# Seven block products for eight in the last MLP pass of a hybrid encoder layer

## The chip, the cores and the metric

The kernel runs on one core of one Trainium2 chip. The metric is the device time in microseconds of one execution. The program has five compute engines that work through their own instruction queues in order: TensorE (PE, with its weight loads shown apart as PEld), VectorE (DVE), ScalarE (ACT), GpSimd (POOL) and SyncE (SP), which in this kernel issues most of the transfers.

## The reference

The input `x` has 2048 tokens of 1024 features, float32. The layer is an RMS norm and a projection into attention (8 heads of 64, three dilation patterns) and a convolution branch, a cross-attention over 256 memory tokens, an MLP, and a closing RMS norm. The part that the change touches is the end:

```python
u = rmsnorm(h, norm_mlp_g[l]) @ w_up[l]            # 1024 -> 4096
h = h + jnp.square(jax.nn.relu(u)) @ w_down[l]     # 4096 -> 1024
return rmsnorm(h, norm_final_g)
```

## The kernel before, in words

Each float32 operand of a large product is split into a high part (rounded to the type that TensorE reads in one pass, `F32R`) and a low part, the difference. A product is then three matmuls, high x high, high x low, low x high. `mm3` (L198 to L201) issues them, one line each, so every large product shows up at L199, L200 and L201. `wsplit2` (L187) makes the two parts of a weight: ScalarE copies the raw weight to the high part (L190), VectorE subtracts (L191).

After a first stage (input projection, convolution and the first attention), the 2048 tokens go through the rest in four passes of 512, `post(p)` (L1219), p = 0 to 3: output projection, cross-attention, MLP, closing norm. While pass p runs, the attention and the convolution of pass p + 1 are woven in between (`weave`, L92 and L1398); pass 3 has nothing woven in. In all passes activations are held by columns: features on the 128 partitions, tokens along the free dimension. The residual stream is eight tiles `hs[m]` of 128 features x 512 tokens.

The MLP of a pass goes in eight groups `fg` of 512 hidden units. For each group:

- four chunks `c` of 128 hidden units. `wpost` (L1089) loads a 512 KB piece of `w_up` and splits it; 8 x 3 matmuls with the weight stationary and 512 tokens streaming give the tile `up`; VectorE applies relu and the norm's factor (L1321), ScalarE squares (L1322) and copies the high part `hhh` (L1323), VectorE makes the low part `hhl` (L1324);
- four pieces of `w_down`, each 512 hidden units x 256 output features, 512 KB, loaded and split the same way. `down` (L1331) makes two tiles `dn` from each, 4 x 3 matmuls per tile, and VectorE adds each to the residual `h` (L1339).

A group is thus 96 matmuls up and 96 down. Raw weights go through two slots (`raw`, two buffers), split weights through four (two in each of two pools, `wp` and `wq`, taken by turns). All weights are issued on SP's queue; a raw slot is free for the next load when the low part has been made from it. The `up` and `dn` tiles take turns in three accumulator banks.

In pass 3 the last group's second product is done in two halves of 256 tokens, so that the closing norm of the first half (`final`, L1354) can go on beside the second. `final` sums the squares over features with matmuls against ones (`rstd_from`, L1170), takes the reciprocal root (`rstd_col`, L169, with GpSimd's power at L177), multiplies by the gain (L1360), turns the tiles by transposes on TensorE (L1367), scales on VectorE or ScalarE (L1371, L1369) and stores.

The order of each queue is not written out by hand alone: a planner takes the program's order and a timeline of its own, and places the instructions and their waits; the order in which `post` and the woven generators yield decides what it sees first.

Of the kernel before, what the change touches and what calls it, by code (L numbers as in the profile page):

```python
# [21 lines left out]
P = 128  # L22
# [21 lines left out]
def f(ap):  # L44
    return ap.bitcast(F32)


def hybrid_layer(ctx, tc, A, out):
# [70 lines left out]
    bscr = dr.tile([KC, P, KC, P], F32, name="bscr")  # L119

# [77 lines left out]
    def mm3(o, lh, ll, rh, rl, first, end):  # L198
        PE.matmul(o, lh, rh, start=first, stop=False)  # L199
        PE.matmul(o, lh, rl, start=False, stop=False)  # L200
        last["pe"] = PE.matmul(o, ll, rh, start=False, stop=end)  # L201
# [894 lines left out]

    wout = {}
# [57 lines left out]
    def ytile(q, k, name, dtype=F32R):  # L1155
        return yp.tile([P, 512], dtype, tag=f"y{q}{k}", name=name)
# [62 lines left out]
    def post(p):  # L1219
# [88 lines left out]
        end = p == NG - 1  # L1308
        for fg in range(FG):
# [16 lines left out]
            if fg == FG - 1:  # L1326
                fsum = ssum_tile(f"f{p}")
                if not end:
                    load_cat(p + 1, 0)

            def down(mp2, t, w, wh, wl):  # L1331
                sl = slice(t, t + w)
                for e in range(2):
                    m = 2 * mp2 + e
                    es = slice(P * e, P * e + P)
                    pt = ps("mm", "dn")[:, 0:w]
                    for k in range(4):
                        mm3(pt, wh[:, k, es], wl[:, k, es], hh["h", k][:, sl], hh["l", k][:, sl], k == 0, k == 3)
                    last["dve"] = DVE.tensor_tensor(hs[m][:, sl], hs[m][:, sl], pt, op=ALU.add)  # L1339
                    if fg == FG - 1:  # L1340
                        add_sq(hs[m][:, sl], fsum[:, sl], m == 0)

            wd = []
            for mp2 in range(4):
                wd.append(wpost(wcols(w_down, mp2 * 256, 256, (4 * fg, 4 * fg + 4)), f"d{p}{fg}_{mp2}", (P, 4, 256)))
                if fg == FG - 1 and end:
                    continue
                down(mp2, 0, 512, *wd[-1])
                yield


        fin = {}

        def final(t, w):  # L1354
            r = rstd_from(fsum[:, t:t + w])
            sl = slice(t, t + w)
            for k in range(KC):
                if t == 0:
                    fin[k] = ytile("h", k, f"fin{p}_{k}", F32)
                DVE.tensor_scalar(fin[k][:, sl], hs[k][:, sl], gain("final", k), None, op0=ALU.mult)  # L1360
            for j in range(w // P):
                c0 = t + P * j
                for g in range(2):
                    ot = ytile("l", 2 * (c0 // P) + g, f"ot{p}{c0}{g}", F32)
                    pt = ps("T", "ot")
                    for i in range(4):
                        PE.transpose(pt[:, P * i:P * i + P], fin[4 * g + i][:, c0:c0 + P], ident)  # L1367
                    if g:
                        ACT.activation(ot, pt, AF.Copy, scale=r[:, j:j + 1])  # L1369
                    else:  # L1370
                        DVE.tensor_scalar(ot, pt, r[:, j:j + 1], None, op0=ALU.mult)  # L1371
                    dma(out[0, 512 * p + c0:512 * p + c0 + P, 512 * g:512 * (g + 1)], ot)
                yield

        if end:
            for t in range(0, 512, 256):
                for mp2 in range(4):
                    down(mp2, t, 256, *wd[mp2])
                yield from final(t, 256)
        else:  # L1380
            load_cat(p + 1, 1)
            yield from final(0, 512)
# [75 lines left out]
```

## Time and profile before

| what | value |
|---|---|
| median of 3 executions | 2888.27 us (2886.27 to 2889.25) |
| the profiled execution | 2888.26 us |
| its span, first to last instruction | 2886.5 us |
| mean granted TensorE clock | 0.994 |
| instructions | 41313 |
| TensorE, VectorE, ScalarE, GpSimd busy | 98%, 64%, 40%, 16% of the span |
| DMA traffic | 433.74 MB, mean 150 GB/s |
| MLP of pass 0, 1, 2, 3 (approximate stretches) | 905 to 1295, 1451 to 1842, 1997 to 2387, 2529 to 2876 us |

Times in a row are microseconds unless marked ns. A row of a group of instructions names line, engine and operation, then what it writes from what it reads, its shapes and count; after the bar come busy time and the mean of one in ns, and then the idle time of the engine before it with what ended that. A matmul's recorded length is longer than its share of TensorE's time, since the next one starts before it ends; counts over a stretch tell the pace. In a row of waits, "A <- B: t, n, m" says that A waited for B t us in total, n times, m at the longest.

### The profile page before, as it was taken

The page shows a single profiled execution, that of the slowest core. Times are in us where ns is not written, and L with a number is a line of the kernel's source. Part 1 is how long each engine was busy: PE and PEld are TensorE (multiplying, and loading weights), DVE is VectorE, ACT ScalarE, POOL GpSimd, SP SyncE. Part 2 cuts the span into 40 slices and gives each one's busy share as a digit, 9 for nine tenths or more (in the row PEclk, how much of TensorE's full clock was granted, in tenths as well). Part 3 has the DMA queues.
Part 4 walks back from the last instruction along what each step waited for, and adds up shares of the span by engine and source line. Part 5 has one row for each costly group of instructions (what it writes and reads, how often), then busy time and mean ns, then how long its engine had stood idle before and what let it go on. Part 6 is the DMA issues. An engine that isn't in the chain of part 4 may idle for free.

```text
span 2886.5 us, 41313 instructions
## 1 busy us (share of the span) xinstructions
PE 2826.6 (98%) x15628; PEld 2376.2 (82%) x15628; DVE 1857.6 (64%) x3306; ACT 1166.3 (40%) x1988; POOL 458.0 (16%) x469
## 2 busy tenths in 40 slices
PE   8999999998999999999999999999999999999999
PEld 7878899887788888888888888888888888888887
DVE  5636535565789776557887765689876555544445
ACT  5633211475554333434543343444333433432233
POOL 1336421122102011200012012002011200000000
PEclk9999999999999999999999999999999999999999
DMA  8979845799734444554444446534543445333332
GB/s 264 295 173 228 202 132 131 182 256 247 205 102 131 135 133 123 168 160 145 121 130 130 138 117 192 175 96 128 142 127 109 139 132 175 93 90 101 96 95 74
DMA packets 598632, 433.74 MB, mean 150 GB/s; under 512 B 191550, under 2 KB 524786, under 8 KB 597921
## 3 DMA queue, kind: packets, MB, share of 16 engines
q1 hardware_dynamic: 558256, 408.21, 50.2%
q10 hardware_dynamic: 37952, 16.88, 2.4%
q0 software_dynamic: 2224, 6.01, 0.6%
q8 instruction: 123, 2.02, 0.3%
q14 instruction: 77, 0.62, 0.1%
HBM read 339.89 MB, written 91.11 MB: 149 GB/s over the span
## 4 chain that ended last, share of the span: by engine, by line
PE 82%; DVE 9%; DMA 5%; issue 2%; ACT 2%; POOL 1%; SPq 1%; POOLq 0%; DVEq 0%; ACTq 0%
PE dn L199 8%; PE dn L200 8%; PE dn L201 8%; PE up L199 7%; PE up L200 7%; PE up L201 7%; PE lin L199 4%; PE lin L201 4%; PE lin L200 4%; DVE cacc L216 3%; PE o L199 2%; PE o L200 2%; PE o L201 2%; PE xs L199 2%; PE xs L201 2%; PE xs L200 2%
## 5 line engine op out<-in xcount | busy, mean ns | idle before, releaser
L199 PE MATMUL dn<-hhh,whi_d 128*128 128x512 f32 (+1 forms) x1056 | 402.8, 392 | 7.2 <-DVE h L1339 6.1
L200 PE MATMUL dn<-hhl,whi_d 128*128 128x512 f32 (+1 forms) x1056 | 403.4, 385 | 1.1 <-DVE hhl L1324 1.1
L199 PE MATMUL up<-mh,whi_u 128*128 128x512 f32 x1024 | 402.9, 393 | 0.5 <-DVE rl L1321 0.5
L201 PE MATMUL dn<-hhh,wlo_d 128*128 128x512 f32 (+1 forms) x1056 | 402.6, 384 | 0.0
L200 PE MATMUL up<-ml,whi_u 128*128 128x512 f32 x1024 | 399.4, 390 | 1.0 <-DVE ml L1214 0.9
L201 PE MATMUL up<-mh,wlo_u 128*128 128x512 f32 x1024 | 399.7, 391 | 0.0
L216 DVE SCALAR_TENSOR_TENSOR cacc<-cu,cw,cacc 128x512 f32<-128x512 f32 x480 | 389.0, 811 | 5.5
L190 ACT CAST whi_d<-raw_d 128x1024 fp32r<-128x1024 f32 x128 | 134.6, 1052 | 418.1 <-PE up L200 378.6
L1339 DVE TENSOR_TENSOR h<-h,dn 128x512 f32<-128x512 f32 (+1 forms) x264 | 172.3, 667 | 162.9 <-PE dn L201 161.7
L190 ACT CAST whi_u<-raw_u 128x1024 fp32r<-128x1024 f32 x128 | 134.4, 1050 | 327.2 <-PE dn L200 304.1
L1321 DVE SCALAR_TENSOR_TENSOR rl<-up,ssumx 128x512 f32<-128x512 f32 x128 | 88.0, 690 | 256.9 <-PE up L201 252.6
L199 PEld LDWEIGHTS dn<-hhh,whi_d 128*128 128x128 f32 x1056 | 198.1, 189 | 47.5 <-DVE h L1339 10.2
L201 PEld LDWEIGHTS dn<-hhh,wlo_d 128*128 128x128 f32 x1056 | 198.8, 188 | 39.7
L200 PEld LDWEIGHTS dn<-hhl,whi_d 128*128 128x128 f32 x1056 | 199.3, 189 | 37.4 <-DVE hhl L1324 2.0
L200 PEld LDWEIGHTS up<-ml,whi_u 128*128 128x128 f32 x1024 | 192.4, 188 | 40.1 <-DVE ml L1214 2.3
L201 PEld LDWEIGHTS up<-mh,wlo_u 128*128 128x128 f32 x1024 | 192.2, 188 | 40.3
L199 PEld LDWEIGHTS up<-mh,whi_u 128*128 128x128 f32 x1024 | 192.4, 188 | 38.5 <-DVE rl L1321 0.9
L774 ACT ACTIVATE sm<-sm,o 128x256 f32<-128x256 f32 (+1 forms) x384 | 160.1, 466 | 126.3 <-DVE o L773 125.9
L773 DVE CUSTOM_DVE_ANT_0 sm<-s,mask 128x256 f32<-128x256 f32 (+1 forms) x384 | 128.5, 375 | 83.5 <-PE s L999 39.4
L191 DVE TENSOR_TENSOR wlo_u<-raw_u,whi_u 128x1024 fp32r<-128x1024 f32 x128 | 158.4, 1237 | 32.7 <-ACT whi_u L190 32.4
L191 DVE TENSOR_TENSOR wlo_d<-raw_d,whi_d 128x1024 fp32r<-128x1024 f32 x128 | 163.2, 1275 | 23.8 <-ACT whi_d L190 23.7
L177 POOL TENSOR_TENSOR nr<-st_v,mhalf 128x4 f32<-128x4 f32 (+1 forms) x13 | 13.0, 997 | 839.2 <-DVE st_v L173 839.2
(403 smaller groups left out, 6320.9 us busy)
## 6 DMA issues: line engine op xcount, KB each, us to landing
raw_u<-in_w_up_dram SPq DMA_DIRECT2D x128, 512.0 KB
raw_d<-in_w_down_dram SPq DMA_DIRECT2D x128, 512.0 KB
raw_o<-in_w_out_dram SPq DMA_DIRECT2D x32, 512.0 KB
raw_a<-ascr SPq DMA_DIRECT2D x32, 512.0 KB
raw_b<-bscr SPq DMA_DIRECT2D x32, 512.0 KB
k<-kscr SPq DMA_DIRECT2D x24, 512.0 KB
k<-kscr SPq DMA_DIRECT2D x8, 1152.0 KB
xn<-in_x_dram SPq DMA_DIRECT2D x32, 256.0 KB
```

The costliest lines, as they stand in the source:

```text
L177: POOL.tensor_tensor(dst, v, mhalf.to_broadcast([P, v.shape[1]]), op=ALU.pow)
L190: ACT.copy(hi, raw)
L191: (lo_eng or DVE).tensor_tensor(lo, raw, f(hi), op=ALU.subtract)
L199: PE.matmul(o, lh, rh, start=first, stop=False)
L200: PE.matmul(o, lh, rl, start=False, stop=False)
L201: last["pe"] = PE.matmul(o, ll, rh, start=False, stop=end)
L216: DVE.scalar_tensor_tensor(acc, u[:, t:t + 512], cw[:, c, t:t + 1], acc, op0=ALU.mult, op1=ALU.add)
L773: last["dve"] = DVE.tensor_tensor_reduce(dst, so, mask[:, 256 * m:256 * m + nk], 1.0, 3e38, ALU.add, ALU.min, mn)
L774: last["act"] = ACT.activation(dst, dst, AF.Exp, bias=mn, scale=-1.0)
L1321: last["dve"] = DVE.scalar_tensor_tensor(r, pt, 0.0, rsb, op0=ALU.max, op1=ALU.mult)
L1339: last["dve"] = DVE.tensor_tensor(hs[m][:, sl], hs[m][:, sl], pt, op=ALU.add)
```

## The change

Three things change.

Pass 3's MLP is a function of its own, `last_mlp`. The sum is held by rows: tokens on the partitions, 1024 features along the free dimension, in two tiles `acc` of four banks' width. The residual's 32 blocks are turned into rows by transposes during the first two chunks of the first group (`to_rows`). In the second product the hidden activations become the stationary operand, and 512 columns of the weight stream.

For the first seven groups, the second product is done as a product of 2 x 2 blocks with seven block products for eight. The activations' blocks are halves of the tokens by halves of the group's hidden units; the weight's are halves of the hidden units by alternate blocks of 128 output features. `parts` makes the activations' blocks and their sums S1 to S4 from each chunk, split into high and low parts. `seven` runs the products in the order A11, A12, S2, S1, S3, S4, A22. Some go on adding in a bank whose content was already added to the rows: the pair of banks X takes A11, S2, S3 and A22, the pair Y takes A12, and the pair Z (the same banks as Y) takes S1 and S4. After each product VectorE adds both tiles of its pair to the rows. The next group's first chunk is computed before the seven products. The eighth group is a plain product, 512 wide, with its rows closed one tile of 128 tokens after another: square and total on ScalarE, reciprocal root, one scaling by factor and gain on VectorE, store from SP's and ScalarE's queues.

The four sums of weight blocks that the seven products need are made in passes 0 to 2: pass p does them for the groups with `fg % 3 == p`, below 7. When a `w_down` piece has been split, VectorE overwrites the raw tile's four blocks with differences, and the tile is written to DRAM (`dscr`). In pass 3 each product's weight is loaded as two transfers of 256 KB, from `w_down` (three of the seven) or from `dscr` (four).

```diff
+    dscr = dr.tile([7, 4, P, 4, 256], F32, name="dscr")
...
+    def wdown(p, fg, m):
+        raw = wp.tile([P, 4, 256], F32, tag="raw", name=f"raw_d{p}{fg}_{m}", bufs=2)
+        dma(raw, wcols(w_down, m * 256, 256, (4 * fg, 4 * fg + 4)))
+        n = turn_w[0]
+        turn_w[0] += 1
+        w = wsplit2(wq if n % 4 > 1 else wp, raw, f"d{p}{fg}_{m}", shape=(P, 4, 256))
+        if fg < 7 and fg % 3 == p:
+            (b11, b12), (b21, b22) = ([raw[:, 2 * a:2 * a + 2, P * b:P * b + P] for b in range(2)] for a in range(2))
+            for o, x, y in ((b11, b12, b11), (b12, b22, b12), (b22, b22, b11), (b21, b21, b22)):
+                DVE.tensor_tensor(o, x, y, op=ALU.subtract)
+            dma(dscr[fg, m], raw)
+        return w
...
+    def last_mlp(hs, y, rsb):
+        FG, p = 8, NG - 1
+        banks.update(up=(4, 5, 6, 7), ux=(0, 1), uy=(2, 3), tr=(0, 1, 2, 3))
+        acc = [xp_.tile([P, 4, 512], F32, tag=f"x{q}0", name=f"rows{q}") for q in "hl"]
+        grow = aq.tile([P, D], F32, tag="ld", name="gain_row")
+        dma(grow, A["norm_final_g"].unsqueeze(0).to_broadcast([P, D]))
...
+        def to_rows(g):
+            t, c = divmod(g, 2)
+            pt = ps("tr", f"hT{g}")
+            for i in range(4):
+                PE.transpose(pt[:, P * i:P * i + P], hs[4 * c + i][:, P * t:P * t + P], ident)
+            ACT.copy(row(t)[:, 512 * c:512 * c + 512], pt)
+
+        def split(t, src):
+            ACT.copy(t[0], src)
+            DVE.tensor_tensor(t[1], src, f(t[0]), op=ALU.subtract)
+
+        def hidden(fg, c):
+            wh, wl = wpost(wcols(w_up, fg * 512 + c * P), f"u{p}{fg}_{c}")
+            pt = ps("up", "up")
+            for k in range(KC):
+                mm3(pt, wh[:, k, :], wl[:, k, :], y["h", k], y["l", k], k == 0, k == KC - 1)
+                if fg == 0 and c < 2 and k % 2:
+                    to_rows(4 * c + k // 2)
+            r = tmp("rl") if c else cv.tile([P, 512], F32, tag="vr", name="rl", bufs=2)
+            last["dve"] = DVE.scalar_tensor_tensor(r, pt, 0.0, rsb, op0=ALU.max, op1=ALU.mult)
+            ACT.activation(r, r, AF.Square)
+            return r
...
+        def parts(rs_, c):
+            r, j = rs_[c], c % 2
+            lo, hi = r[:, 0:256], r[:, 256:512]
+            if c < 2:
+                split([x[:, j] for x in A1], lo)
+                DVE.tensor_tensor(lo, lo, hi, op=ALU.subtract)
+                split([x[:, j] for x in S3], lo)
+            else:
+                r0 = rs_[j]
+                split([x[:, j] for x in A2], r)
+                DVE.tensor_tensor(r0[:, 256:512], r0[:, 256:512], hi, op=ALU.add)
+                DVE.tensor_tensor(r0[:, 0:256], hi, r0[:, 0:256], op=ALU.subtract)
+                split([x[j] for x in S12], r0)
+                DVE.tensor_tensor(lo, lo, r0[:, 0:256], op=ALU.subtract)
+                split([x[:, j] for x in S4], lo)
+
+        def seven(fg):
...
+            for n, (key, w, pts, more, t0, c0) in enumerate((
+                    ("A11", direct(0, 0), X, False, 0, 0), ("A12", direct(1, 0), Y, False, 0, 0),
+                    ("S2", sums(1, 1), X, True, 0, 1), ("S1", sums(0, 0), Z, False, 2, 1),
+                    ("S3", sums(0, 1), X, True, 2, 1), ("S4", direct(1, 1), Z, True, 0, 1),
+                    ("A22", sums(1, 0), X, True, 2, 0))):
+                raw = wp.tile([P, 2, 512], F32, tag="raw", name=f"raw_d{p}{fg}{n}", bufs=2)
+                for j in range(2):
+                    dma(raw[:, j].rearrange("p (m c) -> p m c", m=4), w[j])
...
+                for t in range(2):
+                    for j in range(2):
+                        mm3(pts[t], at[key](0, j, t), at[key](1, j, t), wh[:, j], wl[:, j], not more and j == 0, j == 1,
+                            more)
+                    a = row(t0 + t).rearrange("p (m h c) -> p m h c", m=4, h=2)[:, :, c0, :]
+                    last["dve"] = DVE.tensor_tensor(a, a, pts[t].rearrange("p (m c) -> p m c", m=4), op=ALU.add)
+
+        rs_ = []
+        for fg in range(FG - 1):
+            for c in range(4):
+                if c or not fg:
+                    rs_.append(hidden(fg, c))
+                parts(rs_, c)
+            rs_ = [hidden(fg + 1, 0)]
+            seven(fg)
...
+        for t in range(4):
+            for c in range(2):
+                pt = ps("tr", "dn")
+                for k in range(4):
+                    wh, wl = ws[c][k // 2]
+                    mm3(pt, *(x[:, k, P * t:P * t + P] for x in hh), wh[:, k % 2], wl[:, k % 2], k == 0, k == 3)
+                a = row(t)[:, 512 * c:512 * c + 512]
+                DVE.tensor_tensor(a, a, pt, op=ALU.add)
+                ACT.activation(tmp("sq"), a, AF.Square, accum_out=ss[:, 2 * t + c:2 * t + c + 1])
...
+            rstd_col(r[:, 0:1], sq, 1, top)
+            for c in range(2):
+                a = row(t)[:, 512 * c:512 * c + 512]
+                DVE.scalar_tensor_tensor(a, a, r[:, 0:1], grow[:, 512 * c:512 * c + 512], op0=ALU.mult, op1=ALU.mult)
+                dma(out[0, 512 * p + P * t:512 * p + P * (t + 1), 512 * c:512 * c + 512], a, nc.scalar if c else None)
```

More of the change, by code (lines that the diff above doesn't have):

```diff
@@ L1307, in post @@
         FG = 8
-        end = p == NG - 1
+        if p == NG - 1:
+            last_mlp(hs, y, rsb)
+            return
         for fg in range(FG):
@@ L1327, in post, with down @@
                 fsum = ssum_tile(f"f{p}")
[L1328 to L1332, printed above, removed]
+                load_cat(p + 1, 0)
+            def down(mp2, wh, wl):
                 for e in range(2):
@@ L1352, in post @@
+        r = rstd_from(fsum)
         fin = {}
-        def final(t, w):
-            r = rstd_from(fsum[:, t:t + w])
-            sl = slice(t, t + w)
-            for k in range(KC):
[L1358 to L1373, printed above, removed]
```

81 lines of the change are left out of this document (60 added, 21 removed).

## The prediction

> **What bounds the kernel now.** I read the page first, part 1 and part 4 (the chain that ended last).
>
> ```profile
> PE 2826.6 (98%) x15628; PEld 2376.2 (82%) x15628; DVE 1857.6 (64%) x3306; ACT 1166.3 (40%) x1988; POOL 458.0 (16%) x469
> PE 82%; DVE 9%; DMA 5%; issue 2%; ACT 2%; POOL 1%; SPq 1%; POOLq 0%; DVEq 0%; ACTq 0%
> ```
>
> TensorE is busy 98% of the span and carries 82% of the chain. A share is an average, so the stages come next: the table by stretches, the four MLP stretches in the first four rows (passes 0 to 3), then 100 us inside pass 3, and the two halves of pass 0's MLP.
>
> ```profile
> 905.00:1295.00 390.00, 386.34 (x2001) 319.21 (x2000) 269.35 (x430) 151.20 (x228) 62.31 (x60) 1.00 0.49 141
> 1451.00:1842.00 391.00, 389.48 (x2029) 322.52 (x2027) 270.98 (x436) 152.13 (x229) 62.86 (x61) 1.00 0.49 142
> 1997.00:2387.00 390.00, 386.52 (x2006) 319.28 (x2005) 267.38 (x419) 149.01 (x223) 56.67 (x57) 1.00 0.45 131
> 2529.00:2850.00 321.00, 320.52 (x1415) 263.67 (x1414) 150.80 (x181) 97.78 (x122) 1.01 (x1) 1.00 0.32 95
> 2600.00:2700.00 100.00, 100.00 (x442) 82.36 (x441) 47.60 (x56) 28.82 (x35) 0.00 (x0) 1.00 0.34 100
> 1000.00:1100.00 100.00, 97.58 (x533) 80.81 (x532) 77.39 (x125) 37.32 (x60) 14.30 (x14) 0.98 0.49 138
> 1100.00:1200.00 100.00, 100.00 (x534) 82.99 (x533) 58.24 (x103) 43.23 (x66) 19.20 (x22) 1.00 0.45 133
> ```
>
> Columns: length, then busy time and count on PE, PEld, DVE, ACT, POOL, then granted clock, DMA share, GB/s. Pass 3's MLP runs alone, with TensorE idle 0.5 us in 321, VectorE half idle and the DMA engines at a third. It is paced by the number of matmuls: 442 in 100 us is 0.226 us each (the 0.39 us of a record overlaps the next). The waits of all engines in that stretch say what is late behind TensorE.
>
> ```profile
> ACT whi_u L190 <- PE dn L200: 115.7, 28, 5.5
> PE up L199 <- DVE rl L1321: 0.5, 1, 0.5
> ```
>
> ScalarE, which makes the next weight's high part, waits for TensorE to free a buffer, up to 5.5 us: weights are ready early. So a matmul removed here is time removed, until something else becomes late.
>
> **The change, part by part.**
>
> *Fewer matmuls (a gain).* A group's second product in pass 3 takes 8 tiles x 4 k x 3 = 96 matmuls; as seven block products, 7 x 2 row tiles x 2 k x 3 = 84, again 512 wide. Seven groups lose 12 each: 84 x 0.226 = **-19.0 us**. A group falls from 192 x 0.226 = 43.4 to 180 x 0.226 = 40.7 us. That matmuls fed the other way round (activations stationary, weights streaming) keep this pace is taken from the cross-attention scores, which already run so at the same recorded length (398 ns against 393).
>
> ```profile
> L199 PE MATMUL xs<-whi_a,yh 128*128 128x512 f32 x256 | 101.5, 398 | 0.0
> L199 PE MATMUL up<-mh,whi_u 128*128 128x512 f32 x1024 | 402.9, 393 | 0.5 <-DVE rl L1321 0.5
> ```
>
> *The last group and the close.* Before, the eighth group's second product is 192 matmuls 256 wide, with transposes among them; rows of the timeline:
>
> ```profile
> 2850.69 0.28 PE L199 MATMUL dn<-hhh,whi_d 128*128 128x256 f32 x1
> ...
> 2873.27 1.03 PE L1367 MATMUL ot<-ident,fin 128*128 128x128 f32 x8
> 2874.06 0.36 PE L200 MATMUL dn<-hhl,whi_d 128*128 128x256 f32 x1
> ...
> 2876.05 0.28 PE L201 MATMUL dn<-hhh,wlo_d 128*128 128x256 f32 x1
> 2876.37 0.42 DVE L1339 TENSOR_TENSOR h<-h,dn 128x256 f32<-128x256 f32 x1
> ...
> 2878.46 0.16 DVE L173 TENSOR_SCALAR st_v<-nps 128x2 f32<-128x2 f32 x1 [0.70 <-PE nps L1174]
> ...
> 2880.01 0.75 DVE L1371 TENSOR_SCALAR ot<-ot,nr 128x512 f32<-128x512 f32 x1
> ...
> 2882.36 0.75 DVE L1371 TENSOR_SCALAR ot<-ot,nr 128x512 f32<-128x512 f32 x1 [1.59 <-PE ot L1367]
> ```
>
> First to last start is 25.4 us; 96 matmuls 512 wide take 95 x 0.226 = 21.5: **-3.9**. The 32 turns into rows come instead at the start of pass 3's MLP, among the first two up products: 8 cost 2874.06 - 2873.27 = 0.79 us, so 32 cost **+3.2**. After the last matmul starts, the old close needs 2886.5 - 2876.05 = 10.45 us. The new one: 0.4 until the sum can be read, 0.69 sum, 0.63 square with its total and 0.4 of handovers and adding two totals, 1.55 from the mean to the finished factor (2878.46 to 2880.01, GpSimd's power included), two scalings 1.45, and 3.4 from the start of the last transfer to the end (2882.36 + 0.75 to 2886.5): 8.5, so **-1.9**. It loses the column sums and transposes that wait inside the old close.
>
> *Work on VectorE and the weight ring in pass 3 (cover: TensorE's 40.7 us a group).* Rows of pass 3, by form:
>
> ```profile
> L191 DVE TENSOR_TENSOR wlo_d<-raw_d,whi_d 128x1024 fp32r<-128x1024 f32 x32 | 39.2, 1225 | 11.2 <-ACT whi_d L190 11.2
> L1339 DVE TENSOR_TENSOR h<-h,dn 128x512 f32<-128x512 f32 x56 | 37.2, 686 | 74.4 <-PE dn L201 74.4
> L190 ACT CAST whi_d<-raw_d 128x1024 fp32r<-128x1024 f32 x32 | 33.7, 1054 | 108.7 <-PE up L200 103.2 <-issue 5.5
> L1321 DVE SCALAR_TENSOR_TENSOR rl<-up,ssumx 128x512 f32<-128x512 f32 x32 | 21.9, 691 | 85.1 <-PE up L201 81.7 <-ACT ssumx L1304 3.5
> L1322 ACT ACTIVATE rl<-rl 128x512 f32<-128x512 f32 x32 | 19.9, 625 | 0.0
> L1165 DVE TENSOR_TENSOR ssumf<-ssumf,sq 128x256 f32<-128x256 f32 x14 | 5.9, 423 | 1.5 <-ACT sq L1164 1.4
> ```
>
> Per group VectorE gets 11 low parts x 1.225, 14 sums into the rows x 0.686, 4 relus x 0.69, six 256-wide ops (0.423) for chunks 0 and 1 together, and four 512-wide and eight 256-wide for chunks 2 and 3: 13.5 + 9.6 + 2.8 + 2.5 + 6.1 = 34.5 us of 40.7, 85%. In the seven products alone, 7 x (1.225 + 2 x 0.686) = 18.2 us against 84 x 0.226 = 19.0. That fits with little to spare. ScalarE needs about 20 us.
>
> Each product uses its 512 KB weight for only 12 matmuls, 2.7 us, against 24 matmuls before. The raw weights have two slots; a slot turns in: issue, landing, high part, low part. Landing is bounded by these rows (one weight issued at 2672.81, traffic over before 2677):
>
> ```profile
> 2672.81 16.86 SPq L57 DMA_DIRECT2D raw_u<-in_w_up_dram  x4
> 2674.00:2675.00 1.00, 1.00 (x6) 0.84 (x5) 0.00 (x0) 0.00 (x0) 0.00 (x0) 1.00 0.61 143
> 2675.00:2676.00 1.00, 1.00 (x6) 0.81 (x5) 0.00 (x0) 0.09 (x1) 0.00 (x0) 1.00 1.09 324
> 2676.00:2677.00 1.00, 1.00 (x6) 0.84 (x5) 0.69 (x2) 1.00 (x2) 0.00 (x0) 1.00 0.14 39
> ```
>
> About 3.7 us to land, 0.4 for the second issue (a weight is now two transfers), 1.05 + 0.2 + 1.23: 6.6 us for a slot, 3.3 us for a weight. Needed is 40.7 / 11 = 3.7 on average, and 2.7 within the burst, where four split weights and two raw ones (some 11 us of TensorE work) are in hand. Waits of 0.8 us more per slot would use up the margin. I take **+2** for pass 3; ends 0 and +40 (a slot of 8.5 us: 11 x 8.5 / 2 = 46.8 a group, 6.1 x 7 = 43).
>
> The page "SBUF — State Buffer" of the Trainium skill, section "The DMA setup-cost knee", says that a transfer pays about 2 us however small it is, and advises few large ones. By it two halves one after the other would land in some 5.2 us (my estimate from its fit) and a slot would take 8.1 us, which puts the sum near 2891. The stretch at 2675 moves 324 GB/s, and halves follow each other by one issue, so I expect the fixed parts to overlap.
>
> *Sums of weights in passes 0 to 2 (28 weights).* Four in-place 256-wide differences: 4 x 0.423 = 1.7 us of VectorE each, 47 us in all, then a 512 KB write out of the same raw slot. Cover: TensorE spends 390 / 64 = 6.1 us per weight, VectorE 269 / 64 = 4.2. In the half with the convolution (77.39 of 100) it is 4.7, and 4.7 + 1.7 = 6.4 is over 6.1. That half holds 4 of the 7 groups (0 and 3 of pass 0, 1 of pass 1, 2 of pass 2), so 16 weights run over by 0.3 us, partly within the 2.7 us that a three-bank ring of accumulators allows. The write is queued on SP, where the next raw load and the attention's loads stand behind it.
>
> ```profile
> SPq L57 <- DVE wlo_d L191: 82.2, 23, 6.3
> L191 DVE TENSOR_TENSOR wlo_d<-raw_d,whi_d x31: 1171/1226/2071, 908.0 to 1265.9; 128x1024 fp32r<-128x1024 f32 x31
> PE dn L199 <- DVE h L1339: 2.4, 1, 2.4
> ```
>
> SP already stands up to 6.3 us for a low part (first row, pass 0) without TensorE noticing (third row), and four split weights are worth 24 us, so a slot that turns some 6 us later should be absorbed. I take **+2.5**; ends 0 and +27 (those 16 weights with nothing hidden). Neither term has an end below nothing, as both only add work behind a TensorE that is already full. The planner orders every queue anew, which I price at nothing, with 2 us either way for the range.
>
> *Sum.* -19.0 - 3.9 + 3.2 - 1.9 + 2 + 2.5 = -17.1. The profiled execution took 2888.26 us (span 2886.5, 1.8 around it), equal to the median 2888.27 of the runs. **Forecast 2871 us.**
>
> **The rivals.**
>
> *A, pass 3 bound by the raw slots (slower).* Speaks for it: two slots, half the matmuls per weight, an in-order VectorE at 85%. Against: today's 5.5 us waits of ScalarE, DMA at a third. The gain without it is 21.6 us, 3.1 a group; a group must reach 43.8 us, a slot 8.0 us, before the change loses. At 8.5 us: 2866.7 + 43 + 2.5 = 2912; at 8.2, 45.1 a group, +31 and 2900.
>
> *B, VectorE's handovers pace the burst (no change).* The third, fifth and seventh products add onto banks whose last sums must be read first, and the fourth and sixth reuse the pair of two products earlier. If each of 14 sums costs 0.2 us of waiting, 18.2 + 2.8 = 21.0 against 19.0: +2 a group, 14 in all: 2883; with the chunk chain (relu, square, split) late once a group by 1 us, 2890. Against: a sum has a whole product, 2.7 us, before it is wanted.
>
> *C, the sums disturb passes 0 to 2.* 27 us unhidden gives 2866.7 + 2 + 27 = 2896. For: 6.4 against 6.1; low parts up to 2.07 us where GpSimd works. Against: only 16 weights.
>
> *D, the covers hold entirely.* 2867.
>
> **How the numbers follow.** The forecast with its own range 2864 to 2879: 0.60. D below that or at its edge, 0.05. B or a milder C, 2879 to 2894: 0.20. A, or C in full, above 2894: 0.15. A change under 0.2% (5.8 us) can't be told from none. Faster (under 2882.5): 0.60 + 0.05 + 0.08 of B's = 0.73. Same: 0.10. Slower: 0.17, A and C with the upper end of B's. The range 2862 to 2893 leaves out A and C in full and little else.
>
> **What would show it.** Right: in pass 3 a group lasts 40.7 to 41.2 us, TensorE busy over 98%, 84 matmuls fewer in seven groups, VectorE near 85%, ScalarE's waits for TensorE shorter but there; passes 0 to 2's MLP stretches within 1 us of 390 each. Wrong: TensorE waiting in the seven products for a low part or a raw weight (A), for a sum into the rows (B), or, in passes 0 to 2, for a relu, a residual sum or an attention load (C).

## The result and the profile after

The changed kernel takes 2915.56 us in the median (2910.10 to 2918.73) against 2889.06 for the kernel before in the same series: a ratio of 1.0089 [1.0074, 1.0103]. It is slower by 26.5 us, where 2871 was forecast and 2893 was the upper end of the range. The profiled execution took 2910.39 us, its span 2908.6.

The page of the changed kernel, engines and chain, answers to the first rows of the prediction:

```profile
PE 2841.5 (98%) x15440; PEld 2359.6 (81%) x15440; DVE 1975.3 (68%) x3557; ACT 1206.9 (41%) x2055; POOL 457.1 (16%) x471
PE 80%; DVE 10%; DMA 6%; ACT 2%; issue 1%; SPq 0%; POOL 0%; DVEq 0%; POOLq 0%; ACTq 0%
```

There are 188 matmuls fewer, yet TensorE is busy for 15 us longer. So they must have become slower. The table by stretches: the MLP of passes 0 to 2, that of pass 3, and 100 us inside pass 3.

```profile
900.00:1307.00 407.00, 396.26 (x2000) 320.72 (x1999) 289.36 (x477) 151.67 (x228) 61.02 (x60) 0.98 0.51 150
1468.00:1867.00 399.00, 391.67 (x2003) 320.16 (x2002) 279.92 (x464) 151.68 (x228) 62.45 (x60) 0.99 0.50 147
2028.00:2424.00 396.00, 388.88 (x1984) 317.27 (x1983) 277.17 (x446) 149.56 (x222) 56.36 (x56) 1.00 0.47 140
2571.00:2878.00 307.00, 306.57 (x1333) 249.19 (x1332) 228.64 (x337) 135.78 (x185) 0.00 (x0) 1.00 0.46 135
2700.00:2800.00 100.00, 100.00 (x435) 81.51 (x434) 76.73 (x116) 45.94 (x64) 0.00 (x0) 1.00 0.48 140
```

Two things are seen. In pass 3 TensorE is idle for 0.4 us of 307, so none of the waits that rivals A and B spoke of came; but 100 us hold 435 matmuls where they held 442: 0.230 us each, for 0.226. And the three other passes, some 390 us each before, now take 407, 399 and 396 us for the same 2000 matmuls, with TensorE idle for 7 to 11 us and the mean clock of the first two below 1.

The span can be cut by the first and the last of the small matmuls that sum the squares ahead of each MLP. They are grouped under the tile `ssumx`, with the starts of the first and the last after the three durations. Kernel before:

```profile
L1174 PE MATMUL nps<-ones,ssumx x32: 164/250/250, 901.5 to 2529.6; 128*128 128x1 f32 x32
```

Changed kernel:

```profile
L1191 PE MATMUL nps<-ones,ssumx x32: 164/250/250, 896.4 to 2567.7; 128*128 128x1 f32 x32
```

Up to the first: the head. From the first to the last: passes 0 to 2. From the last to the end: pass 3. Before 901.5 + 1628.1 + 356.9, after 896.4 + 1671.3 + 340.9. Pass 3 gained 16.0 us; passes 0 to 2 lost 43.2.

All runs in one table, cut in the same way (the ratio is to the kernel before on the same chip; where there is no interval, it was one execution). The time is the median of a kernel's executions, the three parts are those of its profiled execution, which took 2910.39 us in the changed kernel, 2894.29 in E1 and 2888.93 in E6:

| run | time, us | ratio | head + passes 0 to 2 + pass 3, us |
|---|---|---|---|
| before | 2889.06 | 1 | 901.5 + 1628.1 + 356.9 |
| changed | 2915.56 | 1.0089 [1.0074, 1.0103] | 896.4 + 1671.3 + 340.9 |
| E1 changed, tiles back in place | 2890.11 | 1.0006 [0.9989, 1.0022] | 902.4 + 1654.6 + 335.5 |
| E2 before, right side 96 bytes down | 2917.49 | 1.0096 [1.0077, 1.0114] | 906.1 + 1645.4 + 362.3 |
| E9 before, right side 64 bytes down | 2902.46 | | 907.9 + 1634.5 + 358.3 |
| E13 before, right 96 down, left 32 up | 2912.77 | | 906.5 + 1643.2 + 361.3 |
| E15 before, both sides 32 up | 2884.67 | | 898.3 + 1627.5 + 357.1 |
| E16 before, left side 96 up | 2913.52 | | 906.5 + 1642.8 + 362.4 |
| E3 E1 without sums and writes | 2866.59 | 0.9919 [0.9898, 0.9939] | 900.7 + 1628.3 + 336.2 |
| E4 E3 with the sums | 2878.74 | 0.9960 [0.9948, 0.9972] | 899.5 + 1640.6 + 336.3 |
| E5 E3 with the writes | 2868.02 | 0.9916 [0.9901, 0.9931] | 897.6 + 1631.8 + 335.8 |
| E6 E1, sums spread | 2883.71 | 0.9974 [0.9962, 0.9987] | 907.6 + 1643.7 + 335.8 |
| E7 E6, sums behind the residual adds | 2883.00 | 0.9966 [0.9954, 0.9979] | 904.2 + 1643.2 + 335.4 |
| E8 E6, write from GpSimd's queue | 2881.99 | 0.9969 [0.9958, 0.9980] | 901.6 + 1647.1 + 335.3 |
| E10 E1, sums in the late groups | 2880.85 | 0.9953 [0.9938, 0.9968] | 901.6 + 1641.9 + 335.6 |
| E11 E10, sums behind the residual adds | 2879.06 | 0.9954 [0.9940, 0.9969] | 903.3 + 1638.2 + 336.0 |
| E14 E11, no sums in pass 1 | 2883.17 | 0.9966 [0.9945, 0.9986] | 903.2 + 1643.0 + 335.5 |
| E17 E11, sums away from the convolution | 2870.33 | 0.9929 [0.9906, 0.9953] | 900.5 + 1629.6 + 335.5 |

The head differs by up to 11.5 us between these profiles; the two other parts carry the argument. Executions of one kernel differ by some 10 us too, E1's by more, so differences of a few us between parts are not told apart by one profile each.

### The profile page after: what moved, and what is told of

Its sections match the earlier page's. It is cut to its first block, busy times and chain, and to the rows that moved or that the text cites. A ratio compares the mean times of both kernels' runs of the same rounds, so it can differ in the third digit from the quotient of the medians.

```text
span 2908.6 us, 41475 instructions
## 1 busy us (share of the span) xinstructions
PE 2841.5 (98%) x15440; PEld 2359.6 (81%) x15440; DVE 1975.3 (68%) x3557; ACT 1206.9 (41%) x2055; POOL 457.1 (16%) x471
## 4 chain that ended last, share of the span: by engine, by line
PE 80%; DVE 10%; DMA 6%; ACT 2%; issue 1%; SPq 0%; POOL 0%; DVEq 0%; POOLq 0%; ACTq 0%
PE dn L201 7%; PE dn L202 7%; PE dn L203 7%; PE up L201 7%; PE up L202 7%; PE up L203 7%; PE lin L201 4%; PE lin L203 4%; PE lin L202 4%; DVE cacc L218 3%; PE o L201 2%; PE o L202 2%; PE xs L201 2%; PE o L203 2%; PE xs L203 2%; PE xs L202 2%
## 5 line engine op out<-in xcount | busy, mean ns | idle before, releaser
L201 PE MATMUL dn<-hhh,whi_d 128*128 128x512 f32 x768 | 304.6, 407 | 18.7 <-DVE h L1356 16.6
L191 ACT CAST whi_d<-raw_d 128x1024 fp32r<-128x1024 f32 x149 | 156.4, 1050 | 371.8 <-PE up L202 257.4
L202 PE MATMUL dn<-hhl,whi_d 128*128 128x512 f32 x768 | 305.8, 400 | 2.8 <-DVE hhl L1343 2.8
L203 PE MATMUL dn<-hhh,wlo_d 128*128 128x512 f32 x768 | 303.6, 397 | 0.0
L192 DVE TENSOR_TENSOR wlo_d<-raw_d,whi_d 128x1024 fp32r<-128x1024 f32 x149 | 187.9, 1261 | 43.9 <-ACT whi_d L191 43.2
L1356 DVE TENSOR_TENSOR h<-h,dn 128x512 f32<-128x512 f32 x192 | 128.5, 682 | 89.0 <-PE dn L203 87.6
L201 PEld LDWEIGHTS dn<-hhh,whi_d 128*128 128x128 f32 x768 | 145.5, 191 | 52.4 <-DVE h L1356 18.8
L202 PEld LDWEIGHTS dn<-hhl,whi_d 128*128 128x128 f32 x768 | 146.7, 191 | 33.3 <-DVE hhl L1343 3.8
L203 PEld LDWEIGHTS dn<-hhh,wlo_d 128*128 128x128 f32 x768 | 146.2, 190 | 33.1
L1340 DVE SCALAR_TENSOR_TENSOR rl<-up,ssumx 128x512 f32<-128x512 f32 x96 | 65.9, 689 | 148.6 <-PE up L203 148.5
```

The source lines that it names most:

```text
L191: ACT.copy(hi, raw)
L192: (lo_eng or DVE).tensor_tensor(lo, raw, f(hi), op=ALU.subtract)
L201: PE.matmul(o, lh, rh, start=first, stop=False, skip_group_check=more)
L202: PE.matmul(o, lh, rl, start=False, stop=False, skip_group_check=more)
L203: last["pe"] = PE.matmul(o, ll, rh, start=False, stop=end, skip_group_check=more)
L1340: last["dve"] = DVE.scalar_tensor_tensor(r, pt, 0.0, rsb, op0=ALU.max, op1=ALU.mult)
```

## Experiments on the pace of the matmuls

The change adds three small tiles (`fin` and two `fsq`) to the pool at the right end of the on-chip memory. In the allocation each takes 32 bytes, and all pools that grow from the right start 96 bytes lower: among them `w_post`, which is `wq` in the code and holds every second pair of split weights (151584 becomes 151488). The pools on the left (`wp` with the other split weights, and the activations that are the other operand) stay. Theory: this move is the slower pace. Rival: the new order of the queues.

**E1** gives the 96 bytes back from the pad tile `tpad`, which nothing reads or writes; the order of every queue is that of the changed kernel. **E2** makes the move in the kernel before, whose queues stay as they are.

```diff
 E1, in the changed kernel
-    top.tile([P, 296], F32, name="tpad")
+    top.tile([P, 272], F32, name="tpad")
 E2, in the kernel before
-    top.tile([P, 296], F32, name="tpad")
+    top.tile([P, 320], F32, name="tpad")
```

> The changed kernel with one number changed: the padding tile at the edge of SBUF is 96 bytes smaller, so that every tile which the three new small tiles had moved by 96 bytes lies where it lay before. The order of all queues is the same as in the changed kernel. Theory P (placement): matmuls whose weights lie in the right-hand weight pool became slower when the pool moved; their start-to-start time goes back from 0.2333 to 0.2267 us, and the time from 2915.6 to about 2887 (2880 to 2893). Rival S (only the sums cost, and the pace is another chip's): the pace stays near 0.231 and the time within 4 us of 2915.

> The kernel before with its padding tile 96 bytes larger and nothing else: same work, same order in all queues, the right-hand tiles 96 bytes lower. Theory P: 2889 becomes 2915 to 2922, with the slow pace on the weights of one of the two pools. Rival S: 2889 within 3 us.

The same stretch of pass 3 as above, E1 and then E2:

```profile
2700.00:2800.00 100.00, 100.00 (x443) 82.81 (x442) 78.75 (x117) 44.95 (x62) 0.00 (x0) 1.00 0.48 139
```

```profile
2700.00:2800.00 100.00, 100.00 (x434) 80.91 (x433) 46.46 (x55) 29.34 (x36) 0.00 (x0) 1.00 0.30 91
```

The pace goes with the 96 bytes and with nothing else: 442 and 443 with the tiles in place, 434 and 435 with them moved, whichever kernel it is. The move alone costs the kernel before 27.3 us of its span (17.3 in passes 0 to 2, 5.4 in pass 3; the 4.6 in the head are within what heads differ by), and E1's pass 3 is shorter than the changed kernel's by the same 5.4 us (340.9 to 335.5). With the move undone the change is no longer slower (1.0006), but not faster either: passes 0 to 2 still have 1654.6 us for 1628.1.

What about the move matters: the start of the right-hand weights, or their distance to the operand on the left? **E9** moves by 64 bytes. **E13** moves the left side too, so that all split weights start at 0 mod 64 bytes; the distance is then 128 less than before. **E15** moves both sides by the same 32 bytes. **E16** leaves the right-hand weights in place and moves the left side up by 96. All are the kernel before, with its order.

```diff
 E9    tpad 296 -> 312
 E13   tpad 296 -> 320, cpad 56 -> 64
 E15   tpad 296 -> 288, cpad 56 -> 64
 E16   cpad 56 -> 80
```

> The kernel before with its padding tile 64 bytes larger (the earlier test had 96) and nothing else. If the pace depends on where an operand lies within 64 bytes, the mean start-to-start of wide matmuls stays at that of the kernel before (0.2268 us in pass 3). If it depends on 128 bytes or more, it rises towards 0.2307.

> Edit: the kernel before with the left pools of weights moved by 32 bytes and the right pools by 96, so that the weights in both pools start at 0 mod 64 bytes; the order of all queues is that of the kernel before. If the absolute start of a weight tile sets the pace of the matmuls, every wide matmul now goes at 0.2333 us or slower (both pools alike) and the run takes 2940 us or more. If it is the distance between tiles on the two sides (weights against activations), moving all together leaves the pace of before, 0.2267 us, and about 2890 us.

> Edit: the kernel before with all pools of both sides moved up by 32 bytes, so that the distances between them stay and every start is at 64 mod 128. If the distance of the weight tile to the tile of the other operand sets the pace, nothing changes: 0.2268 us a matmul in pass 3 and 2885 to 2895 us. If the start of the right-hand weights by itself sets it (32 mod 64 fast, 0 mod 64 slow), 0.2300 or more in pass 3 and 2905 to 2920 us.

> Edit: the kernel before with the left-hand pools (the other operand and half of the weights) moved up by 96 bytes, the right-hand weights where they were. Their distance is then as in the changed kernel. If the distance sets the pace, 0.2300 to 0.2310 us in pass 3 and 2905 to 2920 us, with the right-hand weights alone slow. If the start of the right-hand weights by itself sets it, 0.2268 and 2885 to 2895 us.

The same stretch in E9, E13, E15 and E16, one fence each:

```profile
2700.00:2800.00 100.00, 100.00 (x440) 81.97 (x439) 46.50 (x55) 28.87 (x35) 0.00 (x0) 1.00 0.33 100
```

```profile
2700.00:2800.00 100.00, 100.00 (x435) 81.29 (x434) 46.83 (x56) 28.48 (x35) 0.00 (x0) 1.00 0.32 94
```

```profile
2700.00:2800.00 100.00, 100.00 (x441) 82.41 (x440) 47.55 (x56) 32.22 (x41) 0.00 (x0) 1.00 0.32 95
```

```profile
2700.00:2800.00 100.00, 100.00 (x434) 80.90 (x433) 46.53 (x56) 28.52 (x35) 0.00 (x0) 1.00 0.31 92
```

E15 and E16 decide. With every start changed and the distance kept, the pace stays (441). With the right-hand weights where they were and the other operand 96 bytes away, it falls just as in E2 (434). So it is the distance between a matmul's two operands: 442 at the old distance, 440 at 64 bytes less, 434 at 96 less, 435 at 128 less. No start alone fits: the right-hand weights start at 64 mod 128 bytes in both E2 (151488, slow) and E15 (151616, at the old pace). E9 met neither of its two expectations, since the pace fell only a little. E13 had been meant to hold the distance and did not, so it told these apart no better; its pace fits the distance, and its time lies between the two that were expected. The timeline of E16 in pass 3 shows who pays:

```profile
2639.76 0.39 PE L199 MATMUL up<-mh,whi_u 128*128 128x512 f32 x1
...
2641.80 0.39 PE L199 MATMUL up<-mh,whi_u 128*128 128x512 f32 x1
...
2642.49 0.39 PE L199 MATMUL up<-mh,whi_u 128*128 128x512 f32 x1
...
2651.59 0.39 PE L199 MATMUL up<-mh,whi_u 128*128 128x512 f32 x1
```

From 2639.76 to 2641.80 nine matmuls start, 0.227 us apart; from 2642.49 to 2651.59 it is 39, 0.233 apart. The pace changes between one weight and the next, and the pools take weights two and two. Each wide matmul of pass 3's MLP can be put down to the pool of its weight by the program's order. With a right-hand weight they start 0.2267 us apart in the kernel before and in E15, 0.2289 in E9, 0.2333 in E2 and E16 and 0.2324 in E13; with a left-hand weight 0.2266 to 0.2289 in all six. The recorded length of a matmul (0.39) shows nothing of it: only starts or counts do. Why the distance matters is not settled by these runs.

## Experiments on the sums of weights

E1 keeps 26.5 us of loss in passes 0 to 2. **E3** leaves out the sums and their writes, so that pass 3 works with unsummed weights read from `w_down` (that part of the computation is missing). **E4** makes the 112 subtractions in place and leaves out the writes, **E5** the other way round; pass 3 uses unsummed weights in both. All three start from E1.

```diff
 E3: both removed; E4: the last line; E5: the loop
-            for o, x, y in ((b11, b12, b11), (b12, b22, b12), (b22, b22, b11), (b21, b21, b22)):
-                DVE.tensor_tensor(o, x, y, op=ALU.subtract)
-            dma(dscr[fg, m], raw)
```

> As the padded version, but passes 0 to 2 make no sums of weights and write none; pass 3 loads the four summed weights from w_down unsummed, so the second product of the first seven groups isn't the reference's, with the same transfers and matmuls. Theory P with the stalls in passes 0 to 2 put down to the sums: about 2867 (2863 to 2872), the forecast's gain of 21.6 us; the MLP stretches of passes 0 to 2 within 2 us of those before. Rival A (pass 3 is held up by its weights): above 2880 even so.

> As the version without sums, but VectorE makes the 112 sums in place in passes 0 to 2; nothing is written to DRAM (pass 3 reads unsummed weights, so its second product isn't the reference's). If the raw slot held by the write is what stalls TensorE, the time is near that without sums (2867 to 2873). If VectorE's own time for the sums stalls it, it is near the padded version with sums (about 2884).

> Edit: 96 bytes back, the 28 writes of a piece to the scratch memory stay, the 112 subtractions on VectorE are left out (so pass 3 works with the weights unsummed). With neither, 2866.6 us; with the subtractions alone, 2878.7; with both, 2890.1. If subtractions and writes cost separately, 2876 to 2880 us. If the write costs only because it stands behind a late subtraction, 2867 to 2871 us.

Passes 0 to 2 take 1628.3 us with neither (before: 1628.1), 1640.6 with the subtractions, 1631.8 with the writes, 1654.6 with both. The medians of the whole say the same: 2866.59, 2878.74, 2868.02 and 2890.11. E3 came out as expected, E4 between its two expectations, and E5 as expected if the write costs only behind a late subtraction. The waits of TensorE for a residual add, in E1, E4, E5 and E3, one fence each (total, times, longest):

```profile
PE dn L201 <- DVE h L1356: 16.7, 5, 4.2
```

```profile
PE dn L201 <- DVE h L1355: 10.5, 5, 3.3
```

```profile
PE dn L201 <- DVE h L1353: 7.4, 4, 2.5
```

```profile
PE dn L201 <- DVE h L1351: 6.8, 3, 3.0
```

So the write costs 3.5 us alone and 14.0 behind the subtractions by these profiles (1.4 and 11.4 by the medians). The timeline of the changed kernel around one stall, pass 0's seventh group, shows how:

```profile
1216.61 1.62 DVE L192 TENSOR_TENSOR wlo_d<-raw_d,whi_d 128x1024 fp32r<-128x1024 f32 x1
...
1218.75 1.79 DVE L1110 TENSOR_TENSOR raw_d<-raw_d 128x256 f32<-128x256 f32 x4
...
1220.57 0.33 SPq L57 DMA_DIRECT2D dscr<-raw_d  x1
...
1224.25 0.37 SPq L57 DMA_DIRECT2D raw_d<-in_w_down_dram  x1
...
1228.42 1.05 ACT L191 CAST whi_d<-raw_d 128x1024 fp32r<-128x1024 f32 x1 [3.27 <-DMA raw_d<-in_w_down_dram]
...
1229.50 1.23 DVE L192 TENSOR_TENSOR wlo_d<-raw_d,whi_d 128x1024 fp32r<-128x1024 f32 x1 [1.25 <-ACT whi_d L191]
```

The raw slot now turns in one chain: low part, four subtractions, write (3.7 us until the next load is issued), load (4.2), high part, low part. From the end of the low part (1218.23) to the issue of the next load it is 6.0 us. Without the subtractions the write only reads the slot and can go as soon as the load has landed. What the lateness meets on VectorE follows in the same timeline:

```profile
1231.74 1.34 DVE L1110 TENSOR_TENSOR raw_d<-raw_d 128x256 f32<-128x256 f32 x3
...
1234.27 2.95 DVE L218 SCALAR_TENSOR_TENSOR cacc<-cu,cw,cacc 128x512 f32<-128x512 f32 x2
...
1237.14 1.27 DVE L1356 TENSOR_TENSOR h<-h,dn 128x512 f32<-128x512 f32 x2
...
1237.87 0.80 PE L201 MATMUL dn<-hhh,whi_d 128*128 128x512 f32 x1 [3.78 <-DVE h L1356]
...
1238.46 0.63 PE L202 MATMUL dn<-hhl,whi_d 128*128 128x512 f32 x1
```

Two steps of the convolution's rows (`cacc`) stand ahead of two residual adds on VectorE's in-order queue, at 1.5 us each beside GpSimd's work of the same moment. Only those adds free the accumulator banks, and TensorE stands for 3.78 us. Then its matmuls start 0.43 us apart. The table by stretches over the same stall:

```profile
1234.00:1236.00 2.00, 0.09 (x1) 0.00 (x0) 1.93 (x3) 0.37 (x1) 1.96 (x2) 1.00 0.78 290
1236.00:1238.00 2.00, 0.13 (x1) 0.13 (x1) 2.00 (x3) 1.04 (x1) 0.67 (x1) 0.69 0.04 16
1238.00:1240.00 2.00, 2.00 (x5) 1.61 (x6) 2.00 (x4) 0.00 (x0) 0.00 (x0) 0.50 0.29 65
1240.00:1242.00 2.00, 2.00 (x6) 1.52 (x6) 1.47 (x2) 0.00 (x0) 0.00 (x0) 0.50 1.20 306
```

The granted clock falls to 0.50 in the last part of the stall (0.69 is the mean of that row) and is still there in the two rows behind it. The Trainium skill, page "TensorE: Matmul & The Clock Gate", section "What's actually happening", has the clock halved after an idle window of about 3.4 us, for at least as long; the trace agrees with the ratio and the order of the length, but by the 0.69 the clock fell some 2.7 us into this stall, ahead of a whole window. A stall of 3.8 us thus costs more than 3.8.

The first theory from this was that the sums fall too densely, four pieces in a group, into the busy half of the pass. **E6** spreads them over all groups, **E7** moves them behind the residual adds of their own piece, **E8** issues the write from GpSimd's queue.

```diff
 E6
-        if fg < 7 and fg % 3 == p:
+        if fg < 7 and (fg + m) % 3 == p:
 E7: as E6, and in the loop over the pieces
-                down(mp2, *wdown(p, fg, mp2))
+                w, sums = wdown(p, fg, mp2)
+                down(mp2, *w)
+                sums()
 E8: as E6, and
-            dma(dscr[fg, m], raw)
+            dma(dscr[fg, m], raw, POOL)
```

> The padded version with the sums spread: in passes 0 to 2 every group makes the sums of one or two of its four pieces of w_down (those with (group + piece) mod 3 equal to the pass) where before some groups made all four. The same 28 sums and writes in all. If TensorE stalls because four raw slots in a row are held by sums and writes, the four split weights in hand now cover each one: the MLP stretches of passes 0 to 2 lose 5 us in all and not 28, and the time is about 2869 (2865 to 2876). If each sum and write costs by itself wherever it is, the time stays near the padded version's 2890.

> As the spread version, with the sums of a piece given to the planner after that piece's products and residual adds, not ahead of them. If VectorE's order ahead of the residual adds is what is left of the cost, 1 to 4 us faster than the spread version; if the longer hold of the raw slot counts more, slower than it by as much.

> As the spread version, with the write issued from GpSimd's queue and not from SP's. If the wait of SP for the sums, with raw loads and attention loads behind it, is part of the cost, faster than the spread version by 2 us or more; if only the slot's own turn counts, within 2 us of it.

Spreading brought passes 0 to 2 from 1654.6 to 1643.7, not to within 5 us of 1628.1: the theory falls in this form. E7 (1643.2) and E8 (1647.1) move nothing that can be told from it, so neither SP's queue nor the place of the subtractions within a piece is the main cause. Next, the groups are taken in another order, so that the sums stand late in each pass, two pieces a group (**E10**; **E11** with E7's order of the subtractions).

```diff
-        if fg < 7 and fg % 3 == p:
+        if (fg, m) in SUMS[p]:
...
+    GROUPS = ((5, 6, 7, 0, 1, 2, 3, 4), (3, 4, 7, 5, 6, 0, 1, 2), (0, 1, 2, 7, 3, 4, 5, 6))
...
-        for fg in range(FG):
+        for i, fg in enumerate(GROUPS[p]):
```

> Edit: 96 bytes back, and in each of passes 0 to 2 the groups of the hidden dimension are taken in another order, so that the sums fall in the last five groups of the pass only (two of the four pieces of a group in a pass), where the convolution's rows run on VectorE and GpSimd no more. If the sums cost because they meet the busy first half of a pass (3 us stalls and the half clock behind them), nearly the whole cost goes: 2869 to 2874 us. If each sum and each write costs wherever it stands, it stays at 2882 to 2885 us, as with the sums spread evenly.

> Edit: as e10, and the four subtractions of a piece are emitted behind the residual adds of its own matmuls instead of ahead of them. If the residual adds that queue behind the subtractions are what is left of the stalls, 1 to 3 us less than e10; if not, the same as e10 within 1 us.

E10 missed again, by 7 us; E11 came 1.8 us under it, with the same ratio. But the loss had a place: in E11 passes 0 and 2 were as short as without sums, and pass 1 paid for two stalls at `cacc` steps, one of them in its seventh group. The convolution is not over at half the pass: a last block of it runs in the seventh group of passes 0 and 1. **E14** takes the sums out of pass 1 and puts 16 pieces into pass 0 and 12 into pass 2.

```diff
+    GROUPS = ((5, 6, 7, 3, 4, 0, 1, 2), (0, 1, 2, 3, 4, 5, 6, 7), (0, 1, 2, 7, 3, 4, 5, 6))
+    SUMS = [{(fg, m) for fg in (0, 1, 2) for m in range(4)} | {(fg, m) for fg in (3, 4) for m in (0, 2)}, set()]
...
```

> Edit: as the late groups with the subtractions behind the residual adds, but pass 1 has no sums: 16 pieces in the last five groups of pass 0, 12 in the last four of pass 2. If what is left of the sums' cost is the two stalls of pass 1, 2867 to 2871 us, that is 8 to 12 us less than the run with late groups, and the three passes at 394, 392 and 390 us. If the sums' cost goes by their number, 2877 to 2881 us as before.

Not met either: pass 1 was clean, and pass 0, with sums in its seventh group, paid. The timeline of E14 there is that of the changed kernel over again:

```profile
1236.25 2.95 DVE L218 SCALAR_TENSOR_TENSOR cacc<-cu,cw,cacc 128x512 f32<-128x512 f32 x2
...
1239.13 1.27 DVE L1362 TENSOR_TENSOR h<-h,dn 128x512 f32<-128x512 f32 x2
...
1239.86 0.80 PE L201 MATMUL dn<-hhh,whi_d 128*128 128x512 f32 x1 [3.80 <-DVE h L1362]
```

So the theory now: the sums cost only where such rows stand behind them. **E17** puts none there: passes 0 and 1 make six pieces each at their fifth, sixth and eighth place (the seventh takes the group without sums), pass 2, whose late half has no such rows, makes sixteen in its last four.

```diff
+    GROUPS = ((3, 4, 5, 6, 0, 1, 7, 2), (3, 4, 5, 6, 0, 1, 7, 2), (0, 1, 2, 7, 3, 4, 5, 6))
+    SUMS = [{(fg, m) for fg in gs for m in ms} for gs, ms in (((0, 1, 2), (0, 2)), ((0, 1, 2), (1, 3)), ((3, 4, 5, 6), (0, 1, 2, 3)))]
```

> Edit: as the late groups with the subtractions behind the residual adds, but placed by the trace: in passes 0 and 1 six pieces each at the fifth, sixth and eighth place (the seventh, where a block of the convolution's rows runs, takes the group without sums), in pass 2 sixteen pieces in the last four places. If a sum costs only beside such rows, all three passes take what they take without sums (395, 393 and 390 us, each within 3) and the run 2866 to 2873 us. If the sums' cost goes by their number or by their lateness alone, 2877 to 2883 us.

This was met. Passes 0 to 2 take 1629.6 us, 1.3 more than without any sums, and TensorE waits for residual adds no more than without sums (6.3 us in total, E3 6.8). E17's group of small matmuls, its waits, and pass 2's MLP in the table by stretches:

```profile
L1195 PE MATMUL nps<-ones,ssumx x32: 164/250/250, 900.5 to 2530.1; 128*128 128x1 f32 x32
```

```profile
PE dn L201 <- DVE h L1360: 6.3, 3, 2.4
```

```profile
1997.00:2387.00 390.00, 386.47 (x2002) 318.32 (x2001) 293.55 (x484) 149.19 (x223) 57.70 (x58) 1.00 0.51 153
```

In that pass VectorE is at 293.6 us of 390, more than in any pass of the changed kernel (289.4 of 407), and nothing is lost. So VectorE's mean load over a pass is not what costs. That convolution rows are the only condition is not shown: in E11 two pieces stood in pass 0's seventh group too (eight subtractions from 1208.7 to 1224.9, rows of `cacc` from 1228.5 on), and that pass was as short as without sums. Nor was the new order of groups run without sums. The kernel has the whole change, takes 2870.33 us (2863.82 to 2873.77) and is faster than both, 0.9929 [0.9906, 0.9953] of the kernel before.

## Why the prediction was wrong

**Fewer matmuls, last group and close: right.** The four terms made -21.6. In E1, at the old pace, pass 3 goes from 356.9 to 335.5 us: -21.4. The eighth group's second product takes 21.5 us from first to last start there (2862.6 to 2884.1), as worked out; the seven groups and the turns into rows were not measured one by one. The close, for one, takes 8.4 us from E1's last matmul (start 2884.12) to its end at 2892.5, where 8.5 was worked out.

```profile
2884.12 0.39 PE L203 MATMUL dn<-whi_d,hhl 128*128 128x512 f32 x1
...
2884.46 0.34 ACTq L57 DMA_DIRECT2D out_dram<-rowsl  x1
2884.55 0.69 DVE L1504 TENSOR_TENSOR rowsl<-rowsl,dn 128x512 f32<-128x512 f32 x1
```

**Pass 3's covers: right, and better than taken.** +2 was entered and nothing was paid, so rivals A and B did not happen. A raw slot of E1 in pass 3, from issue to the next issue behind its low part:

```profile
2707.14 1.23 SPq L57 DMA_DIRECT2D raw_d<-in_w_down_dram  x2
...
2711.31 1.05 ACT L191 CAST whi_d<-raw_d 128x1024 fp32r<-128x1024 f32 x1 [2.50 <-DMA raw_d<-in_w_down_dram]
...
2712.39 1.23 DVE L192 TENSOR_TENSOR wlo_d<-raw_d,whi_d 128x1024 fp32r<-128x1024 f32 x1 [1.08 <-ACT whi_d L191]
...
2713.65 0.37 SPq L57 DMA_DIRECT2D raw_u<-in_w_up_dram  x1
```

6.5 us, for 6.6 forecast; ScalarE now waits for a raw weight (2.50 here), as A has it, and TensorE does not. VectorE is busy for 79 us of 100 (E1's row above), where 85% was forecast. The two halves of this weight land within 4.2 us of the first issue, not in the 5.2 that the prediction had worked out from the Trainium skill's page "SBUF — State Buffer", section "The DMA setup-cost knee": the fixed parts were not paid one after the other, and the sum that went with it is refuted for this pass. (By the prediction's own way of counting, a slot of 8.1 us gives 27 us in pass 3 and a sum of 2896, not 2891.)

**Where it failed, first: "keep this pace".** The prediction took 0.226 us for every matmul after the change, and saw in the rearrangement only the planner's order, "which I price at nothing". The order was indeed worth nothing here. But three tiles of 32 bytes moved half of the split weights against the other operand, and the pace of the whole program went with them: 27.3 us of span in E2. No term stood for where tiles come to lie. The pads `tpad` and `cpad` in the code could have raised the question: E1, E2, E15 and E16 change nothing else.

**Where it failed, second: the sums, +2.5.** They cost 26.3 us in passes 0 to 2 (1628.3 to 1654.6). That is near the upper end, +27, which rival C had. VectorE's own price was right: it is busy for 47.8 us more with the sums, where 47 was worked out. E1 and E3, first to last of the small matmuls:

```profile
902.40:2557.00 1654.60, 1627.09 (x8436) 1342.10 (x8435) 1191.39 (x1999) 666.22 (x1052) 201.42 (x202) 0.99 0.48 143
900.70:2529.00 1628.30, 1616.25 (x8437) 1336.28 (x8436) 1143.58 (x1887) 664.32 (x1052) 204.31 (x202) 1.00 0.47 136
```

TensorE is idle for 15.5 us more, of which 9.9 are waits for residual adds (16.7 for 6.8), and busy for 10.8 us more with the same matmuls, at a granted clock of 0.99 for 1.00. The step that failed is "a slot that turns some 6 us later should be absorbed". The lateness was as forecast (6.0 us in the slot above), but the four split weights in hand do not help a TensorE whose accumulator banks wait for an add behind rows of the convolution; and no term stood for the half clock behind a stall. Rival C had the right cost and the right place to look, a wait for a residual sum in passes 0 to 2. Its working, 16 weights that each run over VectorE's load by a little, is not what the trace shows in pass 0's seventh group, which it did not count among the busy ones; how much of the loss in the busy halves goes its way stayed open.

**The sum.** By the medians, pass 3 without sums at the old pace is worth -23.5 us (E3 against its kernel before), the sums +23.5 (E1 against E3) and the move +25.5 (changed against E1): +25.5, where the change measured +26.5. The move made in the kernel before (E2) costs 27.5 by the medians, so the two agree. By the profiles, -21.4 + 26.3 + 27.3 = +32.2, against 22.1 between the two spans. Most of that difference lies in the head, 896.4 us in the changed kernel's profile where 901.5 and the 4.6 of E2 make 906; what sets the head from one execution to the next stayed open.

## What to carry to other kernels

A tile added anywhere moves what is allocated behind it. Before pricing anything else, compare the starts of the matmuls' operands before and after, and count matmuls in a stretch where TensorE is never idle: a loss of two in a hundred there was a matter of place here, not of order. Work that "fits" on an in-order engine by its mean load can cost by what stands behind it in the queue; look for the places where a buffer's release stands behind a long block, and put the extra work elsewhere.

## What the runs showed of the hardware

- The pace of a 128x512 matmul depends on the distance between its two operands in the on-chip memory: 0.227 us or 0.233, by 96 bytes, with all else equal. The steps seen are 0.2267 at the old distance, 0.2289 at 64 bytes less, 0.2333 at 96 less and 0.2324 at 128 less; why is open.
- A VectorE operation with two inputs from on-chip memory took up to 1.42 us, where half of them took 0.42 or less: the 112 sums of the changed kernel (shortest, median, longest in ns), and two stretches in which four of them ran, while GpSimd was busy and while it was idle.

```profile
L1110 DVE TENSOR_TENSOR raw_d<-raw_d x112: 371/422/1419, 899.9 to 2308.4; 128x256 f32<-128x256 f32 x112
```

```profile
1211.00:1216.00 5.00, 5.00 (x23) 4.03 (x23) 4.90 (x5) 1.05 (x1) 4.84 (x5) 1.00 0.12 43
1218.70:1220.50 1.80, 1.80 (x11) 1.53 (x10) 1.70 (x6) 0.00 (x0) 0.00 (x0) 1.00 0.50 96
```

The Trainium skill's page "SBUF — State Buffer", section "Who interferes with whom", says that such an operation contends with a GpSimd instruction that reads the same memory. The trace agrees as far as it goes: the four took 5.0 us beside a busy GpSimd and 1.8 beside an idle one. No run here takes GpSimd's work away.
